# Order of VectorE's low pieces and TensorE's transposes in an expert layer, and the final weight on whole rows

## The chip, the cores and the metric

The kernel runs on one core of one Trainium2 chip. The metric is the device time in microseconds of one execution; the time before is the median of three runs, 1989.85 us (1989.01 to 1989.92). Below, TensorE is the matrix engine (PE in the rows, PEld its weight loads), VectorE is DVE, ScalarE is ACT, GpSimd is POOL, and SP is the queue that issues most transfers.

## What is computed

528 rows of 1024 values (16 meta tokens and 512 inputs) go through one block: a token mixer (retention and mLSTM heads, not touched here), an expert layer, and a final norm. The part that matters:

```python
u = _rmsnorm(h, norm_g)
aff = softmax(u @ w_router)                    # 528 x 16
g, idx = lax.top_k(aff.T, cap)                 # 66 rows for each of 16 experts
xs = u[idx]
hid = silu(xs @ w_gate) * (xs @ w_up)          # 1024 -> 2816
y = (hid @ w_down) * g                         # 2816 -> 1024
h = h.at[idx].add(y)
out = _rmsnorm(h, final_norm_g)[16:]
```

Weights and data are float32. The kernel multiplies in float32r with every operand split into a high and a low piece (the low one is what the high one leaves of the value), and adds three products: high by high, low data by high weight, high data by low weight.

## The kernel before, in words

**Stages.** token_mixer and route fill the first 410 us. Then `experts` goes through the 16 experts, and this takes the rest.

**Data of an expert.** `gather` fetches an expert's 66 rows by an indirect transfer on GpSimd's queue (L903), turns them by eight transposes on TensorE (L910, in two groups of four), and makes the pieces x_h (ScalarE, L916) and x_l (GpSimd, L917). `wide` multiplies them by one half of w_gate or w_up: eight slabs of 128 x 1408, into three banks of PSUM. `gate` puts Silu of the gate's banks into `hid` (ScalarE, L931), `up` multiplies `hid` by the up banks (VectorE, L937, three instructions). `hidden` turns one half of `hid` by eleven transposes (L943, in groups of six and five) and makes the pieces hT (ScalarE L946, VectorE L947). `down` multiplies these by w_down, 16 slabs. `scatter` weighs the result and adds it to the rows in memory, on GpSimd's queue.

**Slabs.** `weights` (L858 to L867) loads a slab into the next of a ring of 22 buffers, from SP's queue but for the loads 21 to 28. `split` makes the pieces of a part of a slab: the high one on ScalarE (L881), the low one on VectorE (L883). `product` issues the three products of each part (L897, L898, L899); only L899 needs the low piece. Pieces have six buffers each for high and low (three in the first expert).

**Order.** The order of an engine's instructions isn't that of the text. A planner simulates the program when it is built and gives each engine, whenever it is free in the simulation, the first instruction of the text that is ready there; on the chip each engine then takes its list strictly in order. `tc.issue_after(x)` forbids the instructions in its block, as far as they are on x's engine, to stand ahead of x in that list. So a transpose can be placed before products that stand ahead of it in the text, unless such an edge forbids it.

In the text, an expert is: gate of half 0, Silu, up of half 0 with its multiplication, two slabs of the gate of half 1, `hidden(hT, 0)`, the rest of that gate, Silu, up of half 1 with its multiplication, three slabs of `down`, `hidden(hT, 1)`, `gather` of the next expert, the rest of `down`, `scatter`. `run(steps, n)` advances such a generator by n slabs.

**The end.** The last expert's down product is made in two halves of 512 columns (`last_down`). `combine(i, o)` adds each half to four tiles of 128 rows held in SBUF, by a product with a matrix that selects rows (L992, L993) and an addition on VectorE (L994), sums the squares on ScalarE (L1054), and forms the norm. For half 0, GpSimd also multiplies the half rows by the final weight (L1057), while TensorE goes on with half 1 of the down product. For half 1, GpSimd adds the sums (L1059) and takes the power (L1060); then VectorE multiplies half 1 by the power and the final weight (L1061), ScalarE scales half 0 by the power (L1062), and SP stores the tile (L1063).

## Time and profile before

| | |
|---|---|
| median of 3 runs | 1989.85 us (1989.01 to 1989.92) |
| the profiled execution's own time | 1988.62 us |
| its span in the trace | 1986.9 us |
| mean granted clock of TensorE | 0.985 of full speed |
| busy: PE, DVE, ACT, POOL | 1936.3, 1688.0, 1450.9, 307.4 us |
| moved by the DMA engines | 604.60 MB, 304 GB/s over the span |

The times of the prediction are set against the profiled execution, because the rows are from it. A matrix product's duration in the rows holds the way through the pipeline, so that durations overlap; what one costs in a stream is the distance between two starts. PEclk is the clock granted to TensorE as a part of its full 2.4 GHz; its lower level is 0.5, 1.2 GHz.

### The profile page before, as it was taken

The numbers are of one execution on the slowest core, as the hardware profiler recorded it, in microseconds if no ns is written. First come the engines' busy times: TensorE is split into PE (matmuls) and PEld (weight loads), VectorE is DVE, ScalarE is ACT, GpSimd is POOL, SyncE is SP. The second block draws the span as 40 slices with busy tenths as digits, with TensorE's granted clock in tenths as the row PEclk, the third lists the DMA queues.
The fourth block names the chain that finished last, engine by engine and source line by source line (L and its number), as shares of the span: only waits on it lengthen the run. The fifth ranks groups of instructions, "written<-read, shape, count | busy, mean of one in ns | idle before, by whom it ended". The sixth has DMA issues, their size and how long they took to land.

```text
span 1986.9 us, 34790 instructions
## 1 busy us (share of the span) xinstructions
PE 1936.3 (97%) x12057; PEld 1513.4 (76%) x12057; DVE 1688.0 (85%) x2614; ACT 1450.9 (73%) x2417; POOL 307.4 (15%) x224
## 2 busy tenths in 40 slices
PE   8999999979999999999999999999999999999997
PEld 7989999767777777777777777777777777777674
DVE  7877776479999999898989888888888888888988
ACT  6565544277878888778777777787878787777776
POOL 1123221210000000030404010401030103030102
PEclk9999998989999999999999999999999999999999
DMA  4322214679999999999999999999999999999973
GB/s 156 98 77 76 65 56 169 233 283 361 373 362 378 352 392 350 363 368 360 376 357 377 352 370 352 382 354 363 360 363 365 353 366 362 371 367 368 344 280 115
DMA packets 134708, 604.60 MB, mean 304 GB/s; under 512 B 18597, under 2 KB 19237, under 8 KB 134531
## 3 DMA queue, kind: packets, MB, share of 16 engines
q1 hardware_dynamic: 123043, 565.28, 75.4%
q10 hardware_dynamic: 6656, 22.29, 3.3%
q0 software_dynamic: 4832, 14.82, 3.0%
q8 instruction: 94, 1.54, 0.3%
q14 instruction: 83, 0.68, 0.1%
HBM read 591.77 MB, written 10.55 MB: 303 GB/s over the span
## 4 chain that ended last, share of the span: by engine, by line
PE 90%; DVE 5%; DMA 2%; issue 1%; ACT 1%; POOL 0%; SPq 0%; POOLq 0%; DVEq 0%; ACTq 0%
PE wide L897 16%; PE wide L898 16%; PE wide L899 16%; PE narrow L899 8%; PE narrow L898 8%; PE narrow L897 8%; PE pj L210 2%; PE pj L211 2%; PE pj L212 2%; PE wide L943 1%; PE narrow L943 1%; DVE left24t L937 1%; PE pj L647 1%; PE pj L649 1%; PE pj L648 1%
## 5 line engine op out<-in xcount | busy, mean ns | idle before, releaser
L898 PE MATMUL wide<-right5t,left29t 128*66 128x512 f32 (+2 forms) x996 | 323.4, 329 | 0.5 <-DVE left29t L917 0.5
L897 PE MATMUL wide<-right5t,left29t 128*66 128x256 f32 (+2 forms) x996 | 316.7, 329 | 1.9 <-ACT left29t L916 1.6
L898 PE MATMUL wide<-left56t,left29t 128*66 128x256 f32 (+2 forms) x988 | 314.8, 326 | 0.0
L897 PE MATMUL wide<-left56t,left29t 128*66 128x256 f32 (+2 forms) x988 | 314.4, 327 | 0.0
L899 PE MATMUL wide<-right5t,left29t 128*66 128x512 f32 (+2 forms) x996 | 254.3, 330 | 0.3 <-DVE right5t L883 0.3
L899 PE MATMUL wide<-left56t,left29t 128*66 128x256 f32 (+2 forms) x988 | 245.4, 327 | 0.0
L897 PEld LDWEIGHTS wide<-left56t,left29t 128*66 128x66 f32 x988 | 135.0, 137 | 48.3 <-ACT left56t L881 1.7
L897 PEld LDWEIGHTS wide<-right5t,left29t 128*66 128x66 f32 x996 | 136.2, 137 | 43.0 <-ACT right5t L881 5.7
L899 PEld LDWEIGHTS wide<-right5t,left29t 128*66 128x66 f32 x996 | 134.6, 138 | 43.5 <-DVE right5t L883 0.7
L917 POOL TENSOR_TENSOR left29t<-right3t,left29t 128x264 fp32r<-128x264 f32 x30 | 155.7, 5206 | 70.6 <-ACT left29t L916 69.9
L899 PEld LDWEIGHTS wide<-left56t,left29t 128*66 128x66 f32 x988 | 132.3, 136 | 38.2
L903 POOL DMA_INDIRECT right3t<-u_rows,right3t x16 | 17.3, 1082 | 926.9 <-PE narrow L899 645.0
L898 PEld LDWEIGHTS wide<-left56t,left29t 128*66 128x66 f32 x988 | 134.5, 136 | 33.4
L898 PEld LDWEIGHTS wide<-right5t,left29t 128*66 128x66 f32 x996 | 136.1, 137 | 23.8 <-DVE left29t L917 0.9
L898 PE MATMUL narrow<-right5t,left55t 128*66 128x512 f32 x443 | 153.6, 352 | 0.0
L897 PE MATMUL narrow<-right5t,left55t 128*66 128x512 f32 x443 | 152.4, 352 | 0.0
L897 PE MATMUL narrow<-left56t,left55t 128*66 128x512 f32 (+1 forms) x441 | 151.4, 349 | 0.0
L210 PE MATMUL pj<-right1t,left2t 128*128 128x256 f32 (+1 forms) x496 | 144.5, 291 | 3.4 <-DVE left23t L387 3.4
L898 PE MATMUL narrow<-left56t,left55t 128*66 128x512 f32 (+1 forms) x441 | 147.6, 349 | 0.0
L211 PE MATMUL pj<-right2t,left2t 128*128 128x256 f32 (+1 forms) x496 | 143.6, 290 | 0.0
L212 PE MATMUL pj<-right1t,left3t 128*128 128x256 f32 (+1 forms) x496 | 143.2, 289 | 0.0
L899 PE MATMUL narrow<-right5t,left55t 128*66 128x512 f32 (+1 forms) x442 | 134.3, 355 | 0.7 <-DVE right5t L883 0.7
(497 smaller groups left out, 5057.6 us busy)
## 6 DMA issues: line engine op xcount, KB each, us to landing
left1t<-in_w_in_f ACTq DMA_DIRECT2D x30, 512.0 KB, 3.9
left43t<-in_w_up SPq DMA_DIRECT2D x12, 704.0 KB, 7.0
left42t<-in_w_up SPq DMA_DIRECT2D x12, 704.0 KB
left48t<-in_w_gate SPq DMA_DIRECT2D x12, 704.0 KB
left47t<-in_w_up SPq DMA_DIRECT2D x12, 704.0 KB, 6.3
left46t<-in_w_up SPq DMA_DIRECT2D x12, 704.0 KB
left25t<-in_w_up SPq DMA_DIRECT2D x12, 704.0 KB
left26t<-in_w_gate SPq DMA_DIRECT2D x12, 704.0 KB, 5.9
```

Of the source, the lines that this page charges most:

```text
L210: nc.tensor.matmul(ps[:, :ln], wh, x_h[:, k, l0:l0 + ln], start=(k == 0), stop=False)
L211: nc.tensor.matmul(ps[:, :ln], wh, x_l[:, k, l0:l0 + ln], start=False, stop=False)
L212: yield nc.tensor.matmul(ps[:, :ln], wl, x_h[:, k, l0:l0 + ln], start=False, stop=(k == KT - 1)).ins
L647: nc.tensor.matmul(ps[:, :ln], h, y_h[:, k, l0:l0 + ln], start=(j == 0), stop=False)
L648: nc.tensor.matmul(ps[:, :ln], h, y_l[:, k, l0:l0 + ln], start=False, stop=False)
L649: nc.tensor.matmul(ps[:, :ln], l, y_h[:, k, l0:l0 + ln], start=False, stop=(j == len(ks) - 1))
L897: nc.tensor.matmul(o, xh, h[:, w], start=start, stop=False)
L898: nc.tensor.matmul(o, xl, h[:, w], start=False, stop=False)
L899: nc.tensor.matmul(o, xh, l[:, w], start=False, stop=last)
L917: (nc.gpsimd if e else nc.vector).tensor_sub(x_l[:, sl], v, x_h[:, sl])
L937: nc.vector.tensor_mul(hid[:CAP, s], b[:CAP, :n], hid[:CAP, s])
L943: nc.tensor.transpose(b[:, j * CAP:(j + 1) * CAP], hid[:CAP, f0 + j:SLAB:RH], ident[:CAP, :CAP])
```

## The change

1. `split` keeps the low pieces' instructions in `lows`, `product` the last product in `latest`.
2. The gate's Silu is called after the first slab of the up product, and the up multiplication after the first slab of what follows (the gate of half 1, or the down product). Its first instruction may not stand ahead of the last low piece but one on VectorE, the others not ahead of the last.
3. `hidden` and `gather` become generators of two groups each. A group's transposes may not stand ahead of the last product in the text so far. `paced` issues one slab of products after each group: `hidden(hT, 0)` goes into the gate of half 1, `hidden(hT, 1)` and `gather(e + 1)` into the down product, each from two slabs on.
4. In the last expert one slab of `last_down` is taken, and its load issued, ahead of the buffers and loads of the final weight and of the rows.
5. In `combine`, GpSimd's L1057 and ScalarE's L1062 go; VectorE multiplies the whole row of 1024 by the power and the final weight in one instruction.

```diff
             with tc.issue_after(ready):
-                nc.vector.tensor_sub(l, src, h)
+                lows.append(nc.vector.tensor_sub(l, src, h).ins)
             return h, l
...
-                    nc.tensor.matmul(o, xh, l[:, w], start=False, stop=last)
+                    latest[0] = nc.tensor.matmul(o, xh, l[:, w], start=False, stop=last).ins
                     c0 += m
+
+        def between():
+
+            return tc.issue_after(latest[0]) if latest[0] else nullcontext()
...
             for g in range(2):
                 b = bank()
-                for j in range(4):
-                    nc.tensor.transpose(b[:, j * CAP:(j + 1) * CAP], xg[:, 4 * g + j::KT], ident[:CAP, :CAP])
+                with between():
+                    for j in range(4):
+                        nc.tensor.transpose(b[:, j * CAP:(j + 1) * CAP], xg[:, 4 * g + j::KT], ident[:CAP, :CAP])
...
                 (nc.gpsimd if e else nc.vector).tensor_sub(x_l[:, sl], v, x_h[:, sl])
+                yield
...
-                nc.vector.tensor_mul(hid[:CAP, s], b[:CAP, :n], hid[:CAP, s])
+                with tc.issue_after(lows[-1 if c else -2]):
+                    nc.vector.tensor_mul(hid[:CAP, s], b[:CAP, :n], hid[:CAP, s])
 
         def hidden(hT, half):
             for f0, fn in ((0, 6), (6, 5)):
                 b = bank("wide" if half else "narrow")
-                for j in range(fn):
-                    nc.tensor.transpose(b[:, j * CAP:(j + 1) * CAP], hid[:CAP, f0 + j:SLAB:RH], ident[:CAP, :CAP])
+                with between():
+                    for j in range(fn):
+                        nc.tensor.transpose(b[:, j * CAP:(j + 1) * CAP], hid[:CAP, f0 + j:SLAB:RH], ident[:CAP, :CAP])
...
                 nc.vector.tensor_sub(hT[:, 1, s], v, hT[:, 0, s])
+                yield
...
+        def paced(steps, *others):
+            for x in others:
+                for _ in x:
+                    run(steps, 1)
+            return run(steps)
+
         hT = None
-        gather(0)
+        run(gather(0))
...
-            g = wide(a["w_gate"], e, 0)
-            gate(run(g))
-            up(run(wide(a["w_up"], e, 0)))
+            g = run(wide(a["w_gate"], e, 0))
+            u = wide(a["w_up"], e, 0)
+            run(u, 1)
+            gate(g)
+            u = run(u)
             g = wide(a["w_gate"], e, 1)
-            run(g, 2)
+            run(g, 1)
+            up(u)
+            run(g, 1)
...
-            hidden(hT, 0)
-            gate(run(g))
-            up(run(wide(a["w_up"], e, 1)))
+            g = paced(g, hidden(hT, 0))
+            u = wide(a["w_up"], e, 1)
+            run(u, 1)
+            gate(g)
+            u = run(u)
+            d = last_down(E - 1, hT, 0) if e == E - 1 else down(e, hT)
+            run(d, 1)
+            up(u)
             if e == E - 1:
                 break
-            d = down(e, hT)
-            run(d, 3)
-            hidden(hT, 1)
-            gather(e + 1)
-            scatter(e, run(d))
+            run(d, 1)
+            scatter(e, paced(d, hidden(hT, 1), gather(e + 1)))
...
-                    nc.gpsimd.tensor_mul(h, h, g_fin[:, s])
                     continue
...
-                nc.vector.scalar_tensor_tensor(h, h, f1, g_fin[:, s], op0=ALU.mult, op1=ALU.mult)
-                nc.scalar.activation(rows[t][:, :512], rows[t][:, :512], AF.Copy, scale=f1)
+                nc.vector.scalar_tensor_tensor(rows[t], rows[t], f1, g_fin, op0=ALU.mult, op1=ALU.mult)
                 nc.sync.dma_start(out[t * P:(t + 1) * P], rows[t])
 
-        d = last_down(E - 1, hT, 0)
-        run(d, 3)
-        hidden(hT, 1)
-        o = run(d)
+        run(d, 1)
+        o = paced(d, hidden(hT, 1))
         d = last_down(E - 1, hT, 1)
```

## Rows read from the trace of the kernel before

**Rows 1.** The page, part 1: engine, busy us, share of the span, instructions

```profile
PE 1936.3 (97%) x12057; PEld 1513.4 (76%) x12057; DVE 1688.0 (85%) x2614; ACT 1450.9 (73%) x2417; POOL 307.4 (15%) x224
```

**Rows 2.** Windows of experts 1-3, 4-14, 5, 7: busy us by engine, PEclk, DMA share, GB/s

```profile
520.10:806.30 286.20, 286.20 (x1711) 215.12 (x1710) 261.21 (x360) 236.76 (x367) 15.21 (x12) 1.00 0.98 370
806.30:1872.70 1066.40, 1063.46 (x6273) 789.27 (x6272) 938.16 (x1321) 836.60 (x1341) 173.18 (x43) 0.99 0.97 364
903.00:999.40 96.40, 96.13 (x572) 71.41 (x571) 85.01 (x120) 75.99 (x123) 21.62 (x4) 1.00 0.97 366
1095.70:1193.60 97.90, 97.63 (x572) 72.37 (x571) 85.42 (x120) 76.30 (x123) 9.72 (x4) 0.98 0.97 362
```

**Rows 3.** The waits (us in total, times, longest): TensorE's, and SP's queue's

```profile
PE wide L943 <- DVE left24t L937: 3.7, 12, 0.7
...
SPq L866 <- DVE left56t L883: 613.2, 386, 14.2
```

**Rows 4.** Order of time, end of expert 7's up products: start, us, engine, line, [idle before]

```profile
1158.22 0.69 DVE L937 TENSOR_TENSOR left24t<-wide,left24t 66x512 f32<-66x512 f32 x1 [1.85 <-PE wide L899]
...
1159.42 1.15 DVE L937 TENSOR_TENSOR left24t<-wide,left24t 66x512 f32<-66x512 f32 x2
...
1160.62 1.55 PE L943 MATMUL wide<-right3t,left24t 66*128 66x66 f32 x11 [0.27 <-DVE left24t L937]
...
1162.01 1.05 PE L910 MATMUL wide<-right3t 66*128 66x66 f32 x8
```

**Rows 5.** Windows: the stretch behind that block of transposes

```profile
1163.00:1166.40 3.40, 3.40 (x14) 2.23 (x13) 3.40 (x8) 3.28 (x8) 2.96 (x2) 0.52 0.89 303
```

**Rows 6.** Order of time, the same place in expert 1

```profile
583.26 0.95 DVE L883 TENSOR_TENSOR left56t<-left25t,left56t 128x768 fp32r<-128x768 f32 x1
...
584.13 1.15 DVE L937 TENSOR_TENSOR left24t<-wide,left24t 66x512 f32<-66x512 f32 x2
...
587.69 1.44 PE L943 MATMUL wide<-right3t,left24t 66*128 66x66 f32 x11
```

**Rows 7.** GpSimd: the page's row of its subtractions, and the fetch of rows (L903)

```profile
L917 POOL TENSOR_TENSOR left29t<-right3t,left29t 128x264 fp32r<-128x264 f32 x30 | 155.7, 5206 | 70.6 <-ACT left29t L916 69.9
...
DMA to landing us min/median/max: 4.8/7.4/15.1
```

**Rows 8.** Order of time, the same place in the last expert

```profile
1937.05 0.34 PE L943 MATMUL wide<-right3t,left24t 66*128 66x66 f32 x1 [0.73 <-DVE left24t L937]
```

**Rows 9.** Order of time, GpSimd's and VectorE's work while the last down product runs

```profile
1960.17 1.33 DVE L883 TENSOR_TENSOR left56t<-left34t,right5t 128x512 fp32r<-128x512 f32 x1
...
1963.73 0.68 DVE L883 TENSOR_TENSOR right5t<-left45t,left56t 128x512 fp32r<-128x512 f32 x1
...
1963.96 1.61 POOL L1057 TENSOR_TENSOR left48t<-left48t,left33t 128x512 f32<-128x512 f32 x1
...
1964.33 1.78 DVE L883 TENSOR_TENSOR left56t<-left45t,left56t 128x512 fp32r<-128x512 f32 x1
```

**Rows 10.** The chain that ended last, in the same stretch: start, us, engine, line

```profile
1963.86 0.44 PE narrow L899
...
1968.47 0.45 PE narrow L899
...
1971.21 0.23 PE narrow L898
```

**Rows 11.** Order of time, the end of the kernel

```profile
1977.85 0.58 POOL L1060 TENSOR_TENSOR right3t<-right3t 128x1 f32<-128x1 f32 x1
...
1978.46 0.75 DVE L1061 SCALAR_TENSOR_TENSOR left32t<-left32t,right3t,left33t 128x512 f32<-128x512 f32 x1
...
1978.67 0.96 POOL L1060 TENSOR_TENSOR right3t<-right3t 128x1 f32<-128x1 f32 x1
...
1982.87 0.33 SPq L1063 DMA_DIRECT2D out<-left47t  x1
```

**Rows 12.** Windows: the half microsecond in which the output's transfers end

```profile
1985.00:1985.50 0.50, 0.00 (x0) 0.00 (x0) 0.00 (x0) 0.00 (x0) 0.00 (x0) 0.50 0.32 123
```

More of the change, by code (lines that the diff above doesn't have):

```diff
@@ L1 @@
 import itertools
-from contextlib import ExitStack
+from contextlib import ExitStack, nullcontext
 import concourse.bass as bass
@@ L882, in split @@
             with tc.issue_after(ready):
-                nc.vector.tensor_sub(l, src, h)
+                lows.append(nc.vector.tensor_sub(l, src, h).ins)
             return h, l
+        latest = [None]
+        lows = []
         def product(slab, f0, cuts, target):
```

## Prediction

> **What bounds the kernel now.** I read the page first, then windows over the experts, then the waits, then the instructions in order of time at the places where the windows differ. The page puts TensorE at 97% busy [rows 1]. Most of the span is the expert stage, in which one expert is 48 slabs of weights times 12 products, and 30 transposes. Cut at the first gate-up product of each expert, the windows fall into two kinds. Experts 1 to 3 take 286.2 us together, 95.40 us each, with TensorE busy without a break [rows 2]. Experts 4 to 14 take 1066.4 us, 96.95 us each: most of them as expert 5 with 96.4, four of them as expert 7 with 97.9 and a granted clock of 0.98 [rows 2]. The work is the same in all of them. So 1066.4 - 11 x 95.40 = 17.0 us are lost in eleven experts, and the question is what the slower ones do otherwise.
>
> The wait list names it: TensorE's transposes of the hidden rows (L943) wait for VectorE's gate-up multiplication (L937) [rows 3]. In order of time, at the end of expert 7's up product: VectorE stands idle for 1.85 us until the last product is done, multiplies the first chunk, and finishes the other two at 1160.57; TensorE then runs 11 transposes, and the 8 of the gather, in one block from 1160.62 to 1163.06 [rows 4]. Behind that block the clock is granted at 0.52, so at the lower of its two levels (1.2 GHz) for most of 3.4 us [rows 5]. That happened behind four of the blocks of this execution, and it is the difference between the 97.9 and the 96.4 us. The rest of the difference (96.4 - 95.4) is the wait ahead of the block and the low pieces, late because VectorE idled and then multiplied. In expert 1, by contrast, VectorE has a low piece of the down weights (L883) right ahead of the multiplication at 584.13, and the transposes come at 587.69 with no wait in front of them [rows 6]. The order that the change writes out is thus already in the trace, three times.
>
> The transfers don't bound it. The queue that loads the slabs waits for VectorE to free a buffer, for hundreds of us in total [rows 3], not for data, and experts 1 to 3 had the faster pace at 370 GB/s [rows 2]. So 95.40 us needs no more than the memory has already given for 286 us.
>
> **The change, part by part.** All of it is set against the profiled execution's own 1988.62 us (span 1986.9, and 1.7 around it); it stands 1.2 us below the median of the runs, 1989.85, less than one fall of the clock.
>
> *Low pieces ahead of the gate-up multiplication, and the calls moved by one slab.* No instruction is added. L937's three multiplications (0.69 + 1.15 us [rows 4]) are put behind the low pieces of the next slab, which VectorE can make while it now idles 1.85 us. Queued behind L937 on VectorE are the low pieces of the slab after that, for which TensorE has a whole slab of products (95.40/48, under 2 us) as cover. ScalarE's Silu moves by the same slab. Those who wait for L937 are the transposes, and these are now pinned behind the second slab, two slabs (some 3.8 us) behind the last up product, against 1.84 us of multiplications: the wait goes, and nothing that I see is late next.
>
> *Paced transposes.* The same 30 transposes per expert, in six groups with a slab of products between them, so no block of 2.4 us. The four falls of the clock go. The gather's transposes come two slabs later; its fetch is issued by the same generator, so it stands later in the text, but it needs only the last reads of the old rows, which end 90 us ahead, and GpSimd has little else to do; it lands in 7.4 us [rows 7]. Were it issued only where it now stands, the pinned transposes, which follow at once, would hold TensorE for up to 7.4 us per expert. The two GpSimd subtractions of 5.2 us each [rows 7] start later too; the last transposes leave ten of the 16 down slabs, 19 us, to cover 10.4. The slab loads keep their order on SP's queue, but in the last expert, where one down slab's load goes ahead of the loads of the final weight and of the rows; with buffers as its only wait I cost it at nothing.
>
> I put experts 4 to 14 at the 95.40 us of experts 1 to 3: **-17.0 us**. Bounds: not below 95.40, since TensorE is busy throughout there; not above expert 5's 96.4 unless a new wait comes. In the last expert TensorE stands idle for 0.73 us ahead of the same transposes [rows 8]: **-0.7**. Experts 0 to 3 stay.
>
> *The final weight, first half.* While the last down product runs, GpSimd multiplies four half rows by the final weight, 1.61 us each, and VectorE's subtraction in that time takes 1.78 us for what takes 0.68 beside no GpSimd work (1.33 at the first of the four) [rows 9]. These two read two operands each from SBUF. The low piece is late and TensorE with it: in the chain two products L899 that waited stand 4.61 us apart with 12 products from one to the other, which at 0.23 us each take 2.76 [rows 10]: 0.92 us lost per multiplication. Three of them and a first one scaled to its smaller stretch (0.65/1.10 of it, 0.54) are 3.3 us. The change takes these four out: **-3.3**. VectorE needs some 0.6 us per piece against 0.69 of TensorE, so the low pieces are in time without them.
>
> *The final weight, last half.* In exchange VectorE multiplies 1024 columns in one go. By size: 768 columns take 0.95 us [rows 6] and 512 take 0.68 [rows 9], 1.05 ns a column; so 0.75 [rows 11] becomes 0.75 + 0.54 = 1.29 us. ScalarE's scaling, as long and beside it, goes for nothing. Two readings of what follows. If only the last product counts, +0.5 us. But the powers on GpSimd (L1060) took 0.58 us when no such product ran and 0.96 when one had started ahead, ending 0.42 us behind that product's end [rows 11]; the products go tile by tile, each released by its own power. Then each of three powers is held up by 0.54 as well: 4 x 0.54 = +2.1 us to the last issue. Some comes back, because the four tiles leave close behind one another now: from the last issue at 1982.87 [rows 11] to the last data at about 1985.2 [rows 12] 2.3 us pass; further apart, the last tile finds the way free, by my estimate 0.2 us sooner. I take **+1.9**, since the stop 0.42 us behind the product's end is in the rows; the ends are +0.5 and +2.1. A gain from this half is excluded: the chain has a longer product and nothing shorter.
>
> The Trainium skill's page SBUF — State Buffer, in Who interferes with whom, says that VectorE with two SBUF inputs and a GpSimd instruction that reads SBUF exclude each other for a whole instruction, and whoever is second is blocked, not slowed. By that rule it is the second reading, +2.1 ahead of the transfer; a reader who takes the two as sharing bandwidth would come out nearer to +0.5. The trace agrees as far as the 0.42 us goes.
>
> Sum: 1988.62 - 17.0 - 0.7 - 3.3 + 1.9 = **1969.5 us**.
>
> **The rivals.** *Only the clock comes back.* The groups are spread and the clock stays up, but the wait moves, to the low pieces of the second slab or to the first gate product of the next expert. Then experts 4 to 14 all take 96.4 as expert 5 does: 1066.4 - 11 x 96.4 = 6.0 us won, with the end 1988.6 - 6.0 - 3.3 + 1.9 = 1981.2. For it: the order is planned ahead, and edges only forbid places in it. Against it: experts 1 to 3.
>
> *The pinned transposes wait, and it is slower.* TensorE takes its queue in order. If VectorE's queue gets the second slab's low pieces ahead of the multiplications too, the transposes behind that slab stand still, with all products behind them. There are two such places per expert, so it decides from (17.0 + 0.7 + 3.3 - 1.9)/30 = 0.64 us at each of 30 places. At one piece of 0.95 us [rows 6] it is 28.5 us against the 19.1 won, 1998 us. For it: the second slab's two low pieces are some 1.6 us. Against it: two slabs of cover, 3.8 us, for 1.84 + 1.6.
>
> *The order does not change.* The plan may come out as before, since the second half's transposes stand behind three slabs in the text even now and were still taken early. Then only the end changes: 1988.6 - 3.3 + 1.9 = 1987.2, within 0.2%. Against it: the new edges forbid just that.
>
> **How the numbers follow.** 0.2% is 4 us, about what a measurement of this kernel can tell from no change. The forecast gets 0.58, the clock alone 0.24, the unchanged order 0.10, the waiting transposes 0.08. Faster: 0.58 + 0.24 = 0.82; same 0.10; slower 0.08. The range starts at 1966, with the end at +0.5, and 2 us for expert 0, whose period I left as it is; it reaches to 1983 to take in the clock alone with 2 us on top. That leaves out the last two cases, 0.18.
>
> **What would show it.** Right: all windows of experts 1 to 14 within 0.3 us of 95.4 and at a clock of 1.00; L943 in groups of 5 or 6; no idle time ahead of them for L937; VectorE's 1.85 us before L937 gone; no subtraction over 1.0 us in the last 30 us; products L1061 of 1.29 us some 1.7 apart, not 1.2. Wrong: waits of TensorE for L937 or L883 of over 0.5 us per expert, a window of 96.4 at full clock, or products L1061 that stay 1.3 apart.

## The result, and the profile after

The changed kernel takes 1974.53 us (median of 4 runs, 1973.48 to 1976.14) against 1989.43 us (4 runs, 1988.08 to 1989.92) of the kernel before: a ratio of 0.9927 (95% interval 0.991 to 0.9944), 14.9 us less. The profiled execution took 1973.48 us (span 1971.8), so the rows below stand 1.05 us under the median.

Line numbers have moved: the products are L900 to L902, the gather's transposes L918, the multiplication L947, the transposes of the hidden rows L954, the power L1083, VectorE's last product L1084.

The page of the changed kernel, part 1, as in [rows 1]:

```profile
PE 1923.2 (98%) x12057; PEld 1512.2 (77%) x12057; DVE 1693.2 (86%) x2614; ACT 1452.3 (74%) x2413; POOL 170.8 (9%) x220
```

The windows of the changed kernel, cut as in [rows 2]: experts 1 to 3, 4 to 14, 5 and 7.

```profile
521.14:806.88 285.74, 285.74 (x1711) 215.06 (x1710) 261.81 (x361) 237.18 (x367) 14.37 (x12) 1.00 0.98 369
806.88:1859.31 1052.43, 1052.43 (x6274) 788.08 (x6272) 944.74 (x1321) 840.70 (x1342) 42.67 (x43) 1.00 0.98 368
902.96:998.60 95.64, 95.64 (x572) 71.61 (x571) 85.84 (x120) 76.42 (x123) 3.93 (x4) 1.00 0.98 369
1094.23:1189.86 95.63, 95.63 (x571) 71.60 (x570) 85.87 (x120) 76.41 (x123) 3.95 (x4) 1.00 0.98 367
```

The two kinds of experts are gone: 5 and 7 take the same time, TensorE is busy throughout, and the clock is granted in full. GpSimd's busy time in experts 4 to 14 went from 173.18 [rows 2] to 42.67 us with 43 instructions in both; the last section comes back to that.

The end of expert 7's up product in order of time, VectorE's multiplications and TensorE's transposes, to be set beside [rows 4]:

```profile
1156.58 0.69 DVE L947 TENSOR_TENSOR left24t<-wide,left24t 66x512 f32<-66x512 f32 x1 [0.65 <-PE wide L902]
1157.18 0.54 DVE L883 TENSOR_TENSOR right5t<-left26t,right5t 128x384 fp32r<-128x384 f32 x1
1157.65 1.14 DVE L947 TENSOR_TENSOR left24t<-wide,left24t 66x512 f32<-66x512 f32 x2
...
1160.97 0.83 PE L954 MATMUL wide<-right3t,left24t 66*128 66x66 f32 x6
...
1163.55 0.77 PE L954 MATMUL wide<-right3t,left24t 66*128 66x66 f32 x5
```

VectorE waits 0.65 us for the last product instead of 1.85, since it makes low pieces until then. The multiplication ends at 1158.79; the first six transposes come 2.2 us later and wait for nothing.

The 12 waits of TensorE for L937 [rows 3] are gone. From expert 1 to the last down product the list of TensorE's waits now has one line, for a low piece in the last expert:

```profile
PE narrow L902 <- DVE right5t L883: 0.7, 1, 0.7
```

The end of the changed kernel in order of time, to be set beside [rows 11]:

```profile
1961.02 0.58 POOL L1083 TENSOR_TENSOR right3t<-right3t 128x1 f32<-128x1 f32 x1
...
1961.63 1.28 DVE L1084 SCALAR_TENSOR_TENSOR left31t<-left31t,right3t,left32t 128x1024 f32<-128x1024 f32 x1
...
1961.84 1.49 POOL L1083 TENSOR_TENSOR right3t<-right3t 128x1 f32<-128x1 f32 x1
...
1963.36 1.28 DVE L1084 SCALAR_TENSOR_TENSOR left48t<-left48t,right3t,left32t 128x1024 f32<-128x1024 f32 x1 [0.45 <-POOL right3t L1083]
...
1968.13 0.33 SPq L1085 DMA_DIRECT2D out<-left46t  x1
```

The first power runs alone and takes 0.58 us; the second starts beside a product and takes 1.49, ending at 1963.33, 0.42 us behind that product's end at 1962.91. The products are 1.73 us apart, and VectorE stands idle between them.

Where the 15.14 us between the two profiled executions lie, from the starts of the first gate product of each expert, the last down product, and the end of the span (us; later kernels are in the same table; "start" is where expert 0's first product begins, "last" runs from expert 15's first product to the last down product, "end" from there to the end of the span):

| kernel | start | expert 0 | 1 to 3 | 4 to 14 | last | end |
|---|---|---|---|---|---|---|
| before | 421.25 | 98.84 | 286.22 | 1066.42 | 100.64 | 13.53 |
| after | 423.22 | 97.92 | 285.74 | 1052.43 | 97.21 | 15.24 |
| transposes_only | 422.91 | 97.89 | 285.74 | 1075.47 | 98.60 | 15.25 |
| unpinned_products | 422.55 | 97.94 | 285.74 | 1075.77 | 98.35 | 15.23 |
| products_only | 422.10 | 97.66 | 286.16 | 1067.87 | 96.76 | 15.23 |
| not_pinned | 423.81 | 98.82 | 285.60 | 1068.04 | 96.76 | 15.23 |
| one_block | 425.26 | 98.13 | 286.16 | 1054.59 | 97.25 | 15.24 |
| end_only | 421.62 | 97.66 | 286.22 | 1066.57 | 97.34 | 15.43 |
| experts_only | 422.18 | 97.93 | 285.74 | 1052.47 | 100.54 | 14.24 |
| weight_in_psum | 422.37 | 97.92 | 285.74 | 1052.47 | 98.34 | 14.15 |
| later_calls | 420.79 | 99.11 | 285.74 | 1052.61 | 97.22 | 15.23 |
| two_powers | 422.43 | 97.94 | 285.74 | 1052.52 | 97.19 | 15.42 |
| later_still | 422.93 | 97.93 | 285.74 | 1050.82 | 97.30 | 15.23 |
| best | 422.84 | 97.94 | 285.74 | 1050.88 | 97.30 | 16.35 |

The start and expert 0 differ from execution to execution by up to 4.5 and 1.5 us; none of the edits touches what stands ahead of the experts. In expert 0 part of that is the clock: in before, not_pinned and later_calls, the three kernels with 98.8 us or more there, it is granted at its lower level (0.50) right at the start of that expert, and in the others it is not. The kernel before, a window as in [rows 2] (the third number from the end is the granted clock):

```profile
422.43:425.84 3.41, 3.27 (x9) 1.94 (x10) 2.03 (x4) 2.37 (x3) 0.00 (x0) 0.50 1.03 425
```

end_only has the same code there, no such stretch, and 97.66 us. So about 1 us of the 15.14 is chance and not the change. The other columns are steady within 0.2 us where the code is the same, but for the end, which holds the landing of the last transfers. So the experiments are read by columns, and the medians beside them.

### The profile page after: what moved, and what is told of

Its sections match the earlier page's. It is cut to its first block, busy times and chain, and to the rows that moved or that the text cites. A ratio compares the mean times of both kernels' runs of the same rounds, so it can differ in the third digit from the quotient of the medians.

```text
span 1971.8 us, 34804 instructions
## 1 busy us (share of the span) xinstructions
PE 1923.2 (98%) x12057; PEld 1512.2 (77%) x12057; DVE 1693.2 (86%) x2614; ACT 1452.3 (74%) x2413; POOL 170.8 (9%) x220
## 4 chain that ended last, share of the span: by engine, by line
PE 91%; DVE 4%; DMA 2%; ACT 1%; issue 1%; POOL 1%; SPq 0%; POOLq 0%; DVEq 0%; ACTq 0%
PE wide L900 16%; PE wide L902 16%; PE wide L901 16%; PE narrow L902 8%; PE narrow L901 8%; PE narrow L900 8%; PE pj L210 2%; PE pj L211 2%; PE pj L212 2%; PE wide L954 1%; PE narrow L954 1%; PE pj L647 1%; PE pj L648 1%; PE pj L649 1%; PE wide L918 1%
## 5 line engine op out<-in xcount | busy, mean ns | idle before, releaser
L900 PE MATMUL wide<-right5t,left29t 128*66 128x256 f32 (+2 forms) x996 | 317.2, 330 | 2.3 <-ACT left29t L924 1.6
L900 PE MATMUL wide<-left56t,left29t 128*66 128x256 f32 (+2 forms) x988 | 314.7, 327 | 0.0
L902 PE MATMUL wide<-right5t,left29t 128*66 128x512 f32 (+2 forms) x996 | 253.4, 329 | 0.3 <-DVE right5t L883 0.2
L902 PE MATMUL wide<-left56t,left29t 128*66 128x256 f32 (+2 forms) x988 | 245.5, 327 | 0.0
L900 PEld LDWEIGHTS wide<-left56t,left29t 128*66 128x66 f32 x988 | 135.0, 137 | 49.6 <-ACT left56t L881 1.7
L900 PEld LDWEIGHTS wide<-right5t,left29t 128*66 128x66 f32 x996 | 138.0, 139 | 43.3 <-ACT right5t L881 6.3
L902 PEld LDWEIGHTS wide<-right5t,left29t 128*66 128x66 f32 x996 | 133.5, 137 | 45.5 <-DVE right5t L883 1.1
L902 PEld LDWEIGHTS wide<-left56t,left29t 128*66 128x66 f32 x988 | 132.3, 136 | 38.0
L900 PE MATMUL narrow<-right5t,left55t 128*66 128x512 f32 x442 | 152.2, 352 | 0.0
L900 PE MATMUL narrow<-left56t,left55t 128*66 128x512 f32 (+1 forms) x442 | 151.8, 347 | 0.0
L901 PE MATMUL narrow<-left56t,left55t 128*66 128x512 f32 (+1 forms) x442 | 146.1, 346 | 0.0
L902 PE MATMUL narrow<-right5t,left55t 128*66 128x512 f32 (+1 forms) x442 | 132.9, 350 | 0.7 <-DVE right5t L883 0.7
L902 PE MATMUL narrow<-left56t,left55t 128*66 128x512 f32 (+1 forms) x442 | 128.3, 345 | 0.0
L210 PEld LDWEIGHTS pj<-right1t,left2t 128*128 128x128 f32 x496 | 96.2, 194 | 4.7 <-issue 2.9
```

Source lines behind the costliest of these rows:

```text
L210: nc.tensor.matmul(ps[:, :ln], wh, x_h[:, k, l0:l0 + ln], start=(k == 0), stop=False)
L900: nc.tensor.matmul(o, xh, h[:, w], start=start, stop=False)
L901: nc.tensor.matmul(o, xl, h[:, w], start=False, stop=False)
L902: latest[0] = nc.tensor.matmul(o, xh, l[:, w], start=False, stop=last).ins
```

## The experiments

The theory: the two parts of the expert change each do what the prediction says of them, and add up with the two terms of the end. The rivals: one of the two parts does all of it and the other is idle; or the parts need each other. Each expectation below names its own. Five kernels take the expert change apart, three the end, four try to go further. Diffs are against the changed kernel unless another is named.

**transposes_only**: transposes pinned and paced, but gate, up and multiplication called as before and no edge for the low pieces.

```diff
-                with tc.issue_after(lows[-1 if c else -2]):
-                    nc.vector.tensor_mul(hid[:CAP, s], b[:CAP, :n], hid[:CAP, s])
+                nc.vector.tensor_mul(hid[:CAP, s], b[:CAP, :n], hid[:CAP, s])
...
-            g = run(wide(a["w_gate"], e, 0))
-            u = wide(a["w_up"], e, 0)
-            run(u, 1)
-            gate(g)
-            u = run(u)
+            g = wide(a["w_gate"], e, 0)
+            gate(run(g))
+            up(run(wide(a["w_up"], e, 0)))
...
```

> Transposes pinned and spread as in the changed kernel, and its end; but the calls of gate, up and down stand as before, and the gate-up multiplication is not pinned behind low pieces. Theory A (the transposes' places do it: taken early and in one block, they wait and let the clock fall): experts 5 to 14 at 95.6 us and a clock of 1.00, time within 2 us of the changed kernel's 1974.5. Rival B (the low pieces ahead of the multiplication do it): the low pieces stay late, windows of about 96.4 us at full clock, 9 us more, some 1983.

Measured: 1997.37 us, ratio 1.0044 (1.0027 to 1.0061), slower than before. Experts 4 to 14 take 1075.47 us, 9 more than before, with the clock granted in full. Neither of the two expected times, 1974.5 and 1983, is near.

**products_only**: the calls and the edge for the low pieces as in the changed kernel, but the transposes neither pinned nor paced.

```diff
-            return tc.issue_after(latest[0]) if latest[0] else nullcontext()
+            return nullcontext()
...
-                for _ in x:
-                    run(steps, 1)
+                run(x)
```

> The other part alone: calls moved by a slab and the multiplication pinned behind low pieces, and the new end; but the transposes are neither pinned nor spread. Theory A: the planner takes the transposes early again, in one block; waits for the multiplication return and the clock falls behind some blocks: windows between 96 and 98 us, 1982 to 1990. Rival B: no waits ahead of the transposes, windows of 95.6 us but for those with a fall of the clock (1.5 us each), about 1980.

Measured: 1988.03 us, ratio 0.9992 (0.9983 to 1.0002), the time of before. It lies in theory A's range, but not by its mechanism: neither a wait for the multiplication nor a fall of the clock came back. With these two runs the idea that the parts add up fell, and with it that one of them does the work: in experts 4 to 14 the first alone costs 9.05 us, the second alone 1.45 (1067.87 against 1066.42, though with a full clock), and both together win 14.0. (Both kernels have the new end, which is why products_only's median is no worse.) The traces say why.

**unpinned_products** has the calls and the transposes of the changed kernel and lacks only the edge that holds the multiplication behind the low pieces.

```diff
-                with tc.issue_after(lows[-1 if c else -2]):
-                    nc.vector.tensor_mul(hid[:CAP, s], b[:CAP, :n], hid[:CAP, s])
+                nc.vector.tensor_mul(hid[:CAP, s], b[:CAP, :n], hid[:CAP, s])
```

> The changed kernel without the edge that puts the multiplication behind the low pieces; the moved calls stay. Theory A: within 1.5 us of the changed kernel, windows of 95.6 us. Rival B: the multiplication goes back ahead of the low pieces, VectorE idles for over 1.5 us ahead of it, windows of 96.4 us, about 1983.

Measured: 1997.16 us, ratio 1.0043 (1.0026 to 1.0059); 1075.77 us in experts 4 to 14, so it is transposes_only over again, outside both expectations, and the moved calls are worth nothing without the edge. unpinned_products in order of time, end of expert 7's up product, VectorE and the TensorE product that waits (the multiplication is L946 here):

```profile
1162.86 0.69 DVE L946 TENSOR_TENSOR left24t<-wide,left24t 66x512 f32<-66x512 f32 x1 [1.85 <-PE wide L902]
1163.47 0.68 DVE L883 TENSOR_TENSOR left56t<-left26t,left56t 128x512 fp32r<-128x512 f32 x1
1164.07 1.15 DVE L946 TENSOR_TENSOR left24t<-wide,left24t 66x512 f32<-66x512 f32 x2
...
1165.87 0.45 PE L902 MATMUL narrow<-right5t,left55t 128*66 128x512 f32 x1 [0.87 <-DVE right5t L883]
```

and its waits from expert 1 to 14:

```profile
PE narrow L902 <- DVE right5t L883: 9.6, 11, 0.9
PE wide L902 <- DVE right5t L883: 4.4, 10, 0.4
```

VectorE idles its 1.85 us as in [rows 4], and the multiplication then pushes the low pieces back. Before, TensorE was busy just then with 19 transposes, 2.4 us in which no low piece was needed: the block that looked like the trouble was also the cover for VectorE. The pin takes that cover away, the products come first and wait for their low piece, about 1.1 us at each of two places per expert (gaps between starts beyond the usual: 0.60 + 0.29 at half 0, 1.03 + 0.16 at half 1).

**not_pinned** has all of the changed kernel, the pacing too, but for the pin.

```diff
-            return tc.issue_after(latest[0]) if latest[0] else nullcontext()
+            return nullcontext()
```

> The changed kernel with its paced groups, its calls and its edge for the multiplications, but with no edge that holds the transposes behind the last product. Theory A (both edges are needed: without the pin the transposes are taken as soon as the plan finds them ready, the low pieces are not the limit any more, and the wait moves to ScalarE's high pieces behind a Silu that waits for TensorE, as when the transposes were neither pinned nor paced): experts 5 to 14 at 97.2 us each, median 1986 to 1990 us, L900 waits of some 1.2 us per expert for L881. Rival B (the place in the text is enough, since a generator stands between the groups): experts 5 to 14 at 95.6, median 1974.5. Rival C (half of it): 96.2 to 96.6, median 1980 to 1984.

Measured: 1989.42 us, ratio 1.0 (0.9991 to 1.001): theory A, and its waits. Experts 4 to 14 and the last one are products_only's within 0.2 us: from expert 4 on, the transposes' place in the text held nothing without an edge. Its waits from expert 1 on:

```profile
PE wide L900 <- ACT right5t L881: 5.6, 10, 0.6
PE wide L900 <- ACT left56t L881: 3.3, 10, 0.3
```

The wait has moved to ScalarE. products_only in order of time, behind the last gate product of expert 7's half 0:

```profile
1111.49 0.59 ACT L940 ACTIVATE left24t<-wide 66x512 f32<-66x512 f32 x1 [4.30 <-PE wide L902]
...
1112.65 0.45 PE L900 MATMUL wide<-right5t,left29t 128*66 128x512 f32 x1 [0.56 <-ACT right5t L881]
...
1115.18 0.45 PE L900 MATMUL wide<-left56t,left29t 128*66 128x512 f32 x1 [0.34 <-ACT left56t L881]
```

ScalarE stands 4.30 us at Silu for the last gate product, with the next high pieces queued behind it. In the changed kernel the same Silu is placed behind more high pieces and stands 2.21 us. The pin acts here through the plan: it changes when the simulation finds TensorE and ScalarE free, and so what stands ahead of Silu. Why the plan comes out just so was not tried.

**one_block** keeps pin and edge, and drops the products between the groups, so that 11 and 8 transposes follow one another.

```diff
-                for _ in x:
-                    run(steps, 1)
+                run(x)
```

> The changed kernel with the transposes pinned, but the groups issued without slabs between them: 19 in one block in the down product, 11 in the gate. Theory A: no waits ahead of the block, but the granted clock falls behind some of the 15 blocks, 1.5 us each; four falls as before make 1980. Rival: the clock fell before because the block stood right behind idle time of TensorE; without that it does not fall, and the time is the changed kernel's 1974.5 within 1.5 us.

Measured: 1976.91 us, ratio 0.9934 (0.9918 to 0.9951). Its transposes at the end of expert 7's up product, and the window of experts 4 to 14:

```profile
1164.30 1.44 PE L954 MATMUL wide<-right3t,left24t 66*128 66x66 f32 x11
...
1165.58 1.05 PE L918 MATMUL wide<-right3t 66*128 66x66 f32 x8
```

```profile
809.55:1864.15 1054.60, 1054.60 (x6274) 787.62 (x6273) 941.56 (x1321) 841.53 (x1342) 47.27 (x43) 1.00 0.97 368
```

The same block as in [rows 4], and the clock is granted in full behind every one: the rival, though the time is 2.4 us above the changed kernel's and not within 1.5. So the block alone does not bring the clock down to its lower level. products_only and not_pinned agree: they have the same 11 and 8 transposes in a row from expert 4 on, no wait ahead of them, and no fall. In before and end_only the block stands behind a wait for the multiplication (0.27 us in [rows 4]), and each has four windows of 97.9 among experts 4 to 14, in different experts. That wait is not enough either: seven of the eleven blocks behind it kept the clock. Pacing itself is worth (1054.59 - 1052.43)/11 = 0.2 us per expert.

**end_only**: the kernel before, with the last part of the change alone.

```diff
-                    nc.gpsimd.tensor_mul(h, h, g_fin[:, s])
...
-                nc.vector.scalar_tensor_tensor(h, h, f1, g_fin[:, s], op0=ALU.mult, op1=ALU.mult)
-                nc.scalar.activation(rows[t][:, :512], rows[t][:, :512], AF.Copy, scale=f1)
+                nc.vector.scalar_tensor_tensor(rows[t], rows[t], f1, g_fin, op0=ALU.mult, op1=ALU.mult)
```

> The kernel before with the new end alone (no GpSimd product, whole rows on VectorE). The sum's terms: -3.3 us while the last down product runs (no subtraction over 1.0 us there, no wait of TensorE for one), +1.7 behind the last product (13.5 us become 15.2). Together 1.6 us less than before, at the edge of what the timing tells; the trace's two stretches decide. If GpSimd's products were not what held VectorE up, the first stretch stays at 100.6 us and the kernel is 1.7 slower than before.

Measured: 1986.65 us, ratio 0.9987 (0.9978 to 0.9996). By columns: last 100.64 to 97.34, so -3.3; end 13.53 to 15.43, so +1.9.

**experts_only**: the changed kernel with the end of before (the same diff the other way round).

> The changed kernel with the old end. The terms: windows of the experts as in the changed kernel (95.6 us), from the start of the last expert to its last product about 100.5 us where the changed kernel has 97.2, and 13.5 us behind it where it has 15.2: 1.6 us more than the changed kernel, 1976.

Measured: 1974.89 us, ratio 0.9928 (0.9915 to 0.9942). Its GpSimd multiplications (L1081 here) and the subtraction beside one of them:

```profile
1947.13 1.61 POOL L1081 TENSOR_TENSOR left48t<-left48t,left32t 128x512 f32<-128x512 f32 x1
1947.51 1.78 DVE L883 TENSOR_TENSOR right5t<-left33t,left56t 128x512 fp32r<-128x512 f32 x1
...
1949.34 0.45 PE L902 MATMUL narrow<-right5t,left55t 128*66 128x512 f32 x1 [0.71 <-DVE right5t L883]
```

[Rows 9] over again, and 3.3 us more in "last". Three of such waits and a smaller one are what the change's last part wins there; at the end it gives back 1.0 by this pair of kernels (15.24 against 14.24) and 1.9 by before and end_only, so that this part is worth 1.4 to 2.3 us. Up to the last issue both pairs agree (9.49 and 9.50 against 11.61, so +2.1); the difference is the landing of the last transfers. The medians, with everything else that varies in them, give 3.1 us (end_only against before) and 0.4 (the changed kernel against this one).

**weight_in_psum** copies the final weight into two banks of PSUM and multiplies half rows by it, so that the products read one operand from SBUF.

```diff
-                nc.vector.scalar_tensor_tensor(rows[t], rows[t], f1, g_fin, op0=ALU.mult, op1=ALU.mult)
+                for j, g in enumerate(weight):
+                    hj = rows[t][:, 512 * j:512 * j + 512]
+                    nc.vector.scalar_tensor_tensor(hj, hj, f1, g, op0=ALU.mult, op1=ALU.mult)
...
+        weight = [bank() for _ in range(2)]
+        for j, g in enumerate(weight):
+            nc.scalar.activation(g, g_fin[:, 512 * j:512 * j + 512], AF.Copy)
```

> The changed kernel, but ScalarE copies the final weight into two PSUM banks and VectorE reads it from there, in two halves a tile, so that its last products read one operand from SBUF and one from PSUM. If the two SBUF operands of the product hold up GpSimd's power: the powers take 0.58 us instead of 1.49, the tiles follow every 1.3 us instead of 1.73, and 15.2 us behind the last product become about 13.5: 1.7 less than the changed kernel. If the power waits for another reason (it is released late, or GpSimd is slow at the second one on), they stay near 1.5 us and the tiles 1.7 apart.

Measured: 1972.7 us, ratio 0.9914 (0.99 to 0.9927). A power beside a product, and the copy that makes room for it:

```profile
1940.73 1.11 ACT L1096 ACTIVATE wide<-left32t 128x512 f32<-128x512 f32 x2
...
1961.95 1.41 DVE L1086 SCALAR_TENSOR_TENSOR left31t<-left31t,right3t,wide 128x512 f32<-128x512 f32 x2
1962.16 0.55 POOL L1083 TENSOR_TENSOR right3t<-right3t 128x1 f32<-128x1 f32 x1
```

The power takes 0.55 us instead of 1.49, though the products are longer (1.40), and the tiles follow every 1.32 us instead of 1.73. That the products are halves is not the reason: products of 512 columns with both operands in SBUF held the power to 0.96 us [rows 11]. So what held the powers up is the two reads from SBUF, and the end is 1.1 us shorter (1.7 were expected). "Last" is 1.1 longer in exchange: TensorE has two new gaps of 0.55 and 0.44 us at 1945.8 and 1947.1, waits for low pieces (L902 for L883). The copies, 1.11 us ahead of them in ScalarE's queue of high pieces, are the likely cause; this was not tried by itself.

**later_calls** puts the scatter's weighing behind the high pieces of the next expert's first gate slab, and one slab more ahead of the last expert's multiplication; **later_still** puts it behind those of two slabs (shown), and the last expert's selection behind the transposes.

```diff
...
-            g = run(wide(a["w_gate"], e, 0))
+            g = wide(a["w_gate"], e, 0)
+            if e:
+                run(g, 2)
+                with tc.issue_after(highs[-1]):
+                    scatter(e - 1, done)
+            g = run(g)
...
```

> The changed kernel with two more moves of the same kind. The weighing of an expert's result (ScalarE, with the scatter) stands behind the high pieces of the next expert's first gate slab, and the last expert takes two down slabs ahead of its multiplication instead of one. In the changed kernel TensorE loses 0.15 us per expert at the first gate slab, waiting for high pieces that stand behind that weighing, and 1.3 us in the last expert for low pieces behind the multiplication. If these are the causes: windows of 95.5 us instead of 95.63 in experts 5 to 14, the last expert 1 us shorter, 2.5 us less in all. If the planner moves the wait elsewhere: windows of 95.6 or more.

Measured: 1972.41 us, ratio 0.9914 (0.99 to 0.9927), but no column differs from the changed kernel's by more than 0.2 us other than the start and expert 0: nothing was won that can be put down to the edit. That the median is 2.1 us lower, near the 2.5 expected, is no sign of it: the profiled execution's gain lies in the start. The weighing still stood ahead of the second slab's high pieces.

> The changed kernel, with the scatter's weighing on ScalarE held behind the high pieces of the next expert's first two gate slabs, and with the last expert's selection written behind the paced transposes. Theory A (the 0.15 us per expert that TensorE still waits for L881 at the second gate slab comes from that weighing, which waits for the last down product): that wait goes, experts 5 to 14 at 95.5 instead of 95.63, 1.3 to 1.5 us less than the changed kernel, ratio 0.992. Rival B (the weighing then stands ahead of other high pieces, or the wait moves to another piece): 95.6 as before, ratio 0.9925. The last expert keeps its wait of 0.7 for a low piece under both, unless the selection stood in its way.

Measured: 1971.67 us, ratio 0.9913 (0.9899 to 0.9927). ScalarE at the start of expert 5 in the changed kernel:

```profile
902.93 1.26 ACT L1012 ACTIVATE left30t<-narrow,right3t 66x512 f32<-66x512 f32 x2 [1.55 <-PE narrow L902]
904.09 1.47 ACT L881 ACTIVATE right5t<-left38t 128x768 fp32r<-128x768 f32 x2
```

and at the start of expert 7 in later_still:

```profile
1092.18 1.47 ACT L881 ACTIVATE right5t<-left48t 128x768 fp32r<-128x768 f32 x2 [0.24 <-PE narrow L902]
...
1093.56 1.24 ACT L1013 ACTIVATE left30t<-narrow,right3t 66x512 f32<-66x512 f32 x2
```

The high pieces now go ahead of the weighing that waits for the last down product, and experts 5 to 14 take 95.48 us instead of 95.63: 1.6 us in experts 4 to 14, theory A. The last expert's wait for a low piece stays, at 1.0 us.

**two_powers** makes the sums and powers of two tiles at a time.

```diff
...
+                if t % 2 == 0:
+                    continue
+                f0, f1 = fin[:, t - 1:t + 1], fin[:, 3 + t:5 + t]
...
-                nc.gpsimd.tensor_tensor(f1, f1, fin[:, 8:9], op=ALU.pow)
-                nc.vector.scalar_tensor_tensor(rows[t], rows[t], f1, g_fin, op0=ALU.mult, op1=ALU.mult)
-                nc.sync.dma_start(out[t * P:(t + 1) * P], rows[t])
+                nc.gpsimd.tensor_tensor(f1, f1, fin[:, 8:10], op=ALU.pow)
+                for r in (t - 1, t):
+                    nc.vector.scalar_tensor_tensor(rows[r], rows[r], fin[:, 4 + r:5 + r], g_fin, op0=ALU.mult, op1=ALU.mult)
+                    nc.sync.dma_start(out[r * P:(r + 1) * P], rows[r])
```

> The changed kernel, with the sums and powers of the last half made for two tiles by one addition and one power on GpSimd (128x2 for two times 128x1), and then two products of VectorE. Theory A (a power is held up until the product beside it has ended, so that each of the last three costs some 0.4 us between two products): only one power is left that can meet a product; the products come in pairs 1.29 apart, the last product to last issue falls from 11.61 us to some 10.3, the median by about 1.3 us to 1973.2 (ratio to the kernel before 0.992). Rival B (the distance of 1.73 us between products is the issue's or VectorE's own): no change, 11.6 us and 1974.5.

Measured: 1972.97 us, ratio 0.9919 (0.9905 to 0.9932). Its sum (L1085) and power (L1086) for the second pair:

```profile
1961.81 1.22 POOL L1085 TENSOR_TENSOR right3t<-right3t 128x2 f32<-128x2 f32 x1 [0.15 <-ACT wide L1078]
...
1963.11 1.61 POOL L1086 TENSOR_TENSOR right3t<-right3t 128x2 f32<-128x2 f32 x1
1964.20 0.34 SPq L1089 DMA_DIRECT2D out<-left48t  x1
1964.76 1.28 DVE L1088 SCALAR_TENSOR_TENSOR left47t<-left47t,right3t,left32t 128x1024 f32<-128x1024 f32 x1 [0.58 <-POOL right3t L1086]
```

A miss of both theories; that the median is near theory A's 1973.2 is luck, since "end" is no shorter (15.42 against 15.24). The pair's products are 1.20 apart, as theory A has it, but the sum meets the first product (1.22 us instead of 0.20 alone), and the power the second, so that the last issue comes 11.44 us behind the last down product instead of 11.61.

**best** joins later_still and two_powers.

> Both of the last two edits together. Theory A: their gains add, 1.3 + 1.4 us less than the changed kernel, ratio 0.9913. Rival B (only the pairs of powers gain): 1.3 us less, ratio 0.992. If neither gains: 0.9927 as the changed kernel.

Measured: 1972.46 us, ratio 0.9912 (0.9898 to 0.9925). Experts 4 to 14 keep their 1050.88, the last issue again comes 11.43 us behind the last product, but the data of the last tiles take 4.9 us to land instead of 3.6, for a reason the runs leave open. later_still is the one version whose gain can be followed in a column; by medians alone the four versions can't be told from one another.

## Why the prediction was right, and where it was off

*Experts 4 to 14, forecast -17.0, measured -14.0.* What was forecast came: no wait for the multiplication, no fall of the clock, all windows alike. The size failed at one term: "I put experts 4 to 14 at the 95.40 us of experts 1 to 3". Experts 5 to 14 take 95.63, 0.23 more, and expert 4 takes 96.08, of which 0.45 is the way the windows are cut (its first product stands ahead of the last two of expert 3, before and after). Of the 0.23 later_still shows 0.15 (95.48): ScalarE's weighing of the scattered rows, ahead of high pieces that TensorE needs. That wait is not new. The kernel before has it too, here at the start of expert 5, to be set beside the changed kernel's lines under later_still:

```profile
902.97 1.26 ACT L1000 ACTIVATE left30t<-narrow,right3t 66x512 f32<-66x512 f32 x2 [1.55 <-PE narrow L899]
904.12 1.46 ACT L881 ACTIVATE right5t<-left38t 128x768 fp32r<-128x768 f32 x2
```

In experts 1 to 3 it is missing: in expert 2 of the kernel before, high pieces start at 614.61 and the weighing behind them, at 617.35. So the good stretches differed from the others by more than the order that the change writes out, and the forecast, which looked for what would be late next among VectorE's low pieces, did not compare ScalarE's queue. The floor itself was not one: experts 1 to 3 went to 95.25.

*The falls of the clock*, some 6 of the 14.0 us (four times 97.9 - 96.4), went as forecast, but not for the reason given. The prediction put them down to the block of transposes, and one_block keeps the block and the clock. What went with the falls is the wait ahead of the block.

*The 96.4 against 95.4 us.* The prediction reads this as "the wait ahead of the block and the low pieces". By the distances between starts on TensorE, expert 5 of the kernel before loses 0.43 us to that wait and 0.15 to the one behind ScalarE's weighing, and nothing to a low piece. Where the rest goes was not found.

*Two parts.* The prediction goes through the low pieces and the transposes one after the other, and does not ask what one does without the other. They are one gain with two halves: in experts 4 to 14 the pinned and paced transposes alone lose 9 us, and the edge with the moved calls alone 1.5.

*The rival of the waiting transposes* was priced at 1998 us and came true at 1997.2 and 1997.4 in the two kernels without the edge, by a wait of about 1.1 us at each of two places per expert, over its break-even of 0.64. Its place was somewhat different: the products ahead of the pinned transposes wait, for low pieces that stand behind the multiplication. What spoke against it, two slabs of cover, holds only with the edge. That the clock alone comes back (1981.2) was not seen in the changed kernel; products_only and not_pinned come nearest, with a full clock and a wait elsewhere, but with 97.2 us per expert where this rival has 96.4. That the order does not change is out: it did.

*GpSimd's product out, -3.3, and the last expert, -0.7.* "Last" went from 100.64 to 97.21, -3.4 instead of -4.0. end_only has the first at -3.3. The second did not come: the wait for L937 is gone, and one for a low piece took its place. The changed kernel in order of time, in the last expert:

```profile
1922.56 0.68 DVE L883 TENSOR_TENSOR right5t<-left33t,right5t 128x512 fp32r<-128x512 f32 x1
1923.16 1.15 DVE L947 TENSOR_TENSOR left24t<-wide,left24t 66x512 f32<-66x512 f32 x2
...
1924.22 1.28 DVE L883 TENSOR_TENSOR right5t<-left45t,left56t 128x512 fp32r<-128x512 f32 x2
...
1924.96 0.45 PE L902 MATMUL narrow<-right5t,left55t 128*66 128x512 f32 x1 [0.74 <-DVE right5t L883]
```

A slab of the half-wide down product there is only two parts of 512, so a multiplication of 1.15 us behind one of its low pieces has less cover than the "whole slab of products" that the prediction counted on.

*The whole rows, +1.9.* Last product to last issue: 1982.87 - 1973.37 = 9.50 before, 1968.13 - 1956.52 = 11.61 after, +2.11, where the second reading had +2.1; the product takes 1.28 us against 1.29 forecast. The landing is 0.40 shorter instead of 0.2, so +1.71. The Trainium skill's page SBUF — State Buffer, section Who interferes with whom, by which VectorE with two SBUF inputs and a reading GpSimd exclude each other for whole instructions, agrees with this, and with weight_in_psum, where one input comes from PSUM and the power is not held up (0.55 us).

*Expert 0 to 3 and the start*, costed at nothing: -1.4 and +2.0 in this pair of executions; both lie within what the table shows from run to run, but for 0.5 us of experts 1 to 3, which is the change's. That they nearly cancel is luck.

Together, profiled against profiled: +3.0 (experts 4 to 14) + 0.6 (last) - 0.2 (end) + 2.0 - 1.4 = 4.0 us over the 1969.5.

## What to carry to other kernels

A block of work that stalls may also be the cover under which another engine catches up: before it is moved, look at what that engine does in the meantime, and move both or neither. In a planned order, a place in the text need not hold without an edge, and an edge on one engine shifts what is late on the next one, so follow the queue of every engine, also of those with slack. A pace taken from a few good stretches of the old trace is an estimate, not a floor, and the good stretches may differ in more than the one thing that was seen: here the changed stretches came out 0.2 us slower and the good ones 0.2 us faster.

## What was not expected of the hardware

GpSimd's subtraction of the gathered rows (two SBUF reads). The kernel before, one engine and tile, experts 4 to 14 (minimum, median, maximum in ns):

```profile
L917 POOL TENSOR_TENSOR left29t<-right3t,left29t x22: 1205/3646/17991, 875.4 to 1849.5; 128x264 fp32r<-128x264 f32 x22
```

and the changed kernel:

```profile
L925 POOL TENSOR_TENSOR left29t<-right3t,left29t x22: 744/768/937, 883.8 to 1840.3; 128x264 fp32r<-128x264 f32 x22
```

The same instruction on the same data takes 0.77 us or up to 18. The prediction took the mean of 5.2 us for its price [rows 7]. It looks like a wait: in expert 7 of the kernel before, the first of two starts at 1164.41, VectorE's instructions follow one another without a gap until one of 0.29 us ahead of 1170.04, and the subtraction, 5.96 us long, ends at 1170.37. VectorE was catching up there. In eight of the eleven experts the first subtraction ends so, 0.3 us behind a gap of VectorE of 0.28 to 0.35 us. In the other three it takes 12.50 us and ends without a gap on record, beside a low piece that takes 1.38 us instead of 0.81; what let it in there is open. Where the clock did not fall behind the block, as in expert 5, TensorE made no pause for VectorE, and GpSimd was busy for 21.62 us instead of expert 7's 9.72 [rows 2]. In transposes_only and products_only it takes 1.0 and 0.9 us on the mean. So a long GpSimd instruction in a trace can be a sign that VectorE is behind, and its duration no price; here it cost nothing, as its cover was long enough.

TensorE's clock fell behind four of eleven blocks of 19 transposes in the kernel before, and in one_block, products_only and not_pinned behind none, with the same block and no wait ahead of it; the prediction had put the falls down to the block. Whether the wait is what it takes was not tried by itself.
